# Early masks, the third pattern's copies and the last normalisation on ScalarE, and quarter turns in another order, in a hybrid encoder layer

## The chip, the cores and the metric

The kernel runs on one core of a Trainium2 chip. A core has five engines that matter here, each with its own queue that it works off in order: TensorE (PE; its weight loads are shown apart as PEld), VectorE (DVE), ScalarE (ACT), GpSimd (POOL) and SyncE (SP), which issues the DMAs. They wait for each other through semaphores. The metric is the device time of one execution in microseconds (us); a profile is one execution seen by the hardware profiler.

## The reference

One encoder layer on 2048 tokens of 1024 features, with three groups of heads. Cut to what matters:

```python
# A: 16 heads of 64, three dilation patterns (window, dilation), each a sliding window
DILATED_PATTERNS = ((128, 1), (512, 4), (2048, 16))
for window, dil in DILATED_PATTERNS:
    o, lse = window_attn(q[:, ::dil], k[:, ::dil], v[:, ::dil], n_side=window // (2 * dil))
out_A = sum(softmax(lse over the 3 patterns) * o)
# B: 8 heads of latent attention, dense over all 2048 keys
out_B = softmax((q_nope @ k_nope + q_rope @ k_rope) * scale) @ v
# M: 4 heads of cross-attention into 256 memory tokens
out_M = softmax(q @ k_mem * scale) @ v_mem
y = concat(RMSNorm_A(out_A), RMSNorm_B(out_B), RMSNorm_M(out_M)) * SiLU(gate)   # 2048 x 2048
h = LayerNorm(ALPHA * h + y @ W_out)                                             # 2048 x 1024
```

In the window attention a query sees the keys at most 64 places away in its subsequence; everything else is set to a large negative number before the softmax. The kernel does this with mask tiles.

## The kernel before, in words

Products that need more than half precision are made from a float16 high part and a float16 low part (`ph` and `pl`, `yh` and `yl`, `woh` and `wol`): the high part is a rounded copy, the low part a subtraction.

**Start, to 1367 us.** `embed` normalises the input and transposes it, then come the projections and gates, one long row of matmuls, and the memory attention.

**Dilated stage, about 1376 to 1757 us.** For each of 16 heads, `head_units` yields 10 units: four for the first pattern (`unit1`), four for the second (`unit2`), two for the third (`unit3`). A unit is a score tile of 128x1024 (a mask is added on PE by a product with `ident_b`, L1810, and the scores by L1819), one or two exponentials on ACT (`probabilities`, L1465 gives `pf`, L1476 or L1470 or DVE's L1472/L1478 gives `ph`), a subtraction for `pl` on DVE or POOL (L1473/L1479), edge masks on POOL (L1761), and the products with the values (`attend`, L1486 to L1488) into a PSUM tile `ps_o`, of which there are two. `Out.add` collects six row blocks in such a tile (at the end four) and copies it out (L1791) to the stage tile `so`, three copies to each pattern and head; a PSUM tile can be filled again only after its copy. `g` is the pattern, 0 to 2. The masks (`mask_tile`, `keep`, L1707 to L1736) are made by POOL: 5 memsets (L1708) and 28 affine selects (L1714), for the tiles `in`, `ed` (two each) and `diag`.

**Latent stage, 1757 to 2464 us.** For each of 8 heads and 4 query blocks (h, n) there are 8 units k2: six score matmuls (L1619 to L1621), two exponentials on ACT, `pl` on the engine that `lo_eng` picks (every third on POOL, else DVE), and 48 value matmuls; pairs of units are pushed together. Beside them run the maxima of a block to come: a matmul into `ps_x` (L1567) and a reduction on DVE (L1573) for each, two to a unit. At k2 = 6 of the blocks n = 1, 2, 3 of the first heads, `low` makes one 128x1024 piece of the output weight's low part on DVE (`wol`, L1984), 16 in all.

**Last stage, 2461 to 2846 us.** 16 output tiles of 128 tokens. `Prep` of a tile loads and merges the heads' results, takes the sums of squares (ACT, L2049), the roots (DVE, ACT, `rsqrt`) and normalises three groups of columns (`normalise`, L2060, DVE). `turn` then takes a quarter of 512 columns: four transposes on PE (L2068), the product with the gate (DVE, L2072), the high part (ACT, L2073) and the low part (DVE, L2074). Then 96 matmuls make the output tile (L2094), and `Post` adds the residual and normalises (L2142 to L2159).

The order of the work: in the latent and the last stage the code runs under `in_order`, so every engine's queue has the instructions in the order in which the code issues them, and the lists `planned` and `pipe` decide at which step a piece is issued. Outside such regions a scheduler places instructions; where the masks' instructions stand is its choice.

Of the kernel before, what the change touches and what calls it, by code (L numbers as in the profile page):

```python
# [16 lines left out]
ALU = mybir.AluOpType  # L17
# [45 lines left out]
def tile_layer(ctx: ExitStack, tc: tile.TileContext, x, mem, pos, invf, sgn, g_embT, b_embT, g_emb, b_emb, w_in,  # L63
# [175 lines left out]
    def value_block(vpool, chunks, vnat, unscale, dst, w, vt_bufs=1, both=False):  # L239


        amax = vpool.tile([P, NQ], F32, tag="vmx", name="v_amax")
        vt = vpool.tile([P, S], F32, tag="vt", bufs=vt_bufs, name="v_t")
        for n in range(NQ):
            ps = chunks(n)
            nc.scalar.activation(vt[:, n * 512:(n + 1) * 512], ps, AF.Copy, scale=w.un)
            nc.vector.tensor_reduce(out=amax[:, n:n + 1], in_=vt[:, n * 512:(n + 1) * 512], axis=AX.X, op=ALU.max,
                                    apply_absolute_value=True)
        am = vpool.tile([P, 4], F32, tag="vam", name="v_am")
        nc.vector.tensor_reduce(out=am[:, 0:1], in_=amax, axis=AX.X, op=ALU.max)  # L250
        nc.vector.tensor_scalar(out=am[:, 1:2], in0=am[:, 0:1], scalar1=1e-30, scalar2=None, op0=ALU.max)
        nc.vector.tensor_scalar(out=am[:, 0:1].bitcast(I32), in0=am[:, 1:2].bitcast(I32), scalar1=0x7F800000,
                                scalar2=None, op0=ALU.bitwise_and)
        nc.vector.tensor_scalar(out=am[:, 2:3], in0=am[:, 0:1], scalar1=2.0 ** -13, scalar2=None, op0=ALU.mult)
        nc.vector.reciprocal(am[:, 3:4], am[:, 2:3])
        nc.vector.tensor_copy(unscale, am[:, 2:3])
        vh = vpool.tile([P, S], F16, tag="vh", bufs=1, name="v_h")
        vl = vpool.tile([P, S], F16, tag="vl", bufs=1, name="v_l")
        for n in range(NQ):
            c = slice(n * 512, (n + 1) * 512)  # L260
            nc.scalar.activation(vh[:, c], vt[:, c], AF.Copy, scale=am[:, 3:4])
            nc.vector.scalar_tensor_tensor(out=vl[:, c], in0=vt[:, c], scalar=am[:, 3:4], in1=vh[:, c],
                                           op0=ALU.mult, op1=ALU.subtract)
        def turn(half, src, o):
            def go():
                pt = ps_x(F16)
                for i in range(8):
                    t = half * 8 + i
                    nc.tensor.transpose(pt[:, i * P:(i + 1) * P], src[:, t * P:(t + 1) * P], ident_h)
                vo, pv = vnat[:, half * 8:half * 8 + 8, :, o:o + 64], pt[:].rearrange("p (t h e) -> p t h e", t=8, h=2)  # L270
                if both and o == 0:
                    nc.vector.tensor_copy(vo, pv)
                else:
                    nc.scalar.copy(vo, pv)
                if half == 1 and o and dst is not None:
                    dst_t = dst.rearrange("(t p) c -> p t c", p=P)
                    nc.sync.dma_start(out=dst_t[:, 0:NT], in_=vnat[:].rearrange("p t h c -> p t (h c)"))
                    nc.sync.dma_start(out=dst_t[:, NT:], in_=vnat[:, 0:WRAP // P].rearrange("p t h c -> p t (h c)"))
            return go

        return [turn(half, src, o) for half in range(2) for src, o in ((vh, 0), (vl, 65))]


    early = ExitStack()
    sets, msets, vsets = [None, None], [None, None], [None, None]
    with ExitStack() as p1:
# [478 lines left out]
        with tc.tile_pool(name="nz", bufs=1, reuse_waits="tile", side="right") as nz, tc.tile_pool(name="sk", bufs=2, reuse_waits="tile", side="right") as sk:  # L765
            norms = nz.tile([P, 2, 8], F32, bufs=1, name="norms")
            powers = nz.tile([P, 2, 8], F32, bufs=1, name="powers")
            kscale = nz.tile([P, 8], F32, bufs=1, name="kscale")
            qscale = nz.tile([P, 8], F32, bufs=1, name="qscale")
            hbound = nz.tile([P, 1], F32, bufs=1, name="hbound")  # L770
            ones_b = nz.tile([P, 1], BF16, bufs=1, name="ones_b")
            same_head = nz.tile([P, P], F32, bufs=1, name="same_head")
            with tc.tile_pool(name="p0", bufs=1, side="right") as p0, in_order(*EALL):
                embed(p0)
            nc.sync.dma_start(out=gO, in_=g_outT)
            gain_powers()
            tables()
            plain(False, range(5, 8))
            with tc.tile_pool(name="ro", bufs=1, reuse_waits="tile", side="right") as ro:
                rotary(False)  # L780
                query_scales()
                with tc.tile_pool(name="sl", bufs=2, reuse_waits="tile", side="right") as sl:
                    plain(True, range(2, 8))
                    rotary(True)
# [809 lines left out]
    def latent_units(h):  # L1594
# [62 lines left out]
        for n in range(NQ):  # L1657
            for k2 in range(8):
                if (n, k2) == (0, 0 if h else 2):
                    begin()  # L1660
                if n and len(wol) < NT:
                    if k2 == 0:
                        raws.append(load_raw(la, len(woh), 1))
                    if k2 == 4:
                        high(raws[0])
                    if k2 == 6:
                        low(raws.pop())
                yield unit(n, k2)
# [13 lines left out]
                            ended.append((heads[h], m))  # L1682
                        yield

    lo_turn = [0]

    def lo_eng():
        lo_turn[0] += 1
        return nc.gpsimd if lo_turn[0] % 3 == 0 else nc.vector

    raws, planned = [], {}
# [10 lines left out]
    da = p3.enter_context(tc.tile_pool(name="da", bufs=2, reuse_waits="tile"))  # L1702
    ascale = da.tile([P, AH], F32, bufs=1, name="ascale")
    nc.sync.dma_start(out=ascale, in_=ascale_d)

    def mask_tile(name):
        t = da.tile([P, 512], BF16, bufs=1, name=name)  # L1707
        nc.gpsimd.memset(t, 0.0)  # L1708
        return t

    def keep(t, c0, shape, coef, base, cm):

        v = t[:, c0:c0 + shape[0] * shape[1]].rearrange("p (a b) -> p a b", a=shape[0])
        nc.gpsimd.affine_select(out=v, in_=v, pattern=[[coef[0], shape[0]], [coef[1], shape[1]]], base=base,  # L1714
                                channel_multiplier=cm, compare_op=ALU.is_ge, fill=NEG)

    masks = {}
    for pat, shape, coef in ((1, (16, 8), (1, 16)), (2, (4, 32), (1, 4))):
        neg = (-coef[0], -coef[1])
        inner = mask_tile(f"in{pat}")  # L1720
        edge = mask_tile(f"ed{pat}")
        for c0 in (0, 256):
            keep(inner, c0, shape, coef, 0, -1)
            keep(inner, c0 + 128, shape, neg, 0, 1)

        keep(edge, 0, shape, neg, 0, 1)
        keep(edge, 0, shape, (0, 0), -64, 1)
        keep(edge, 128, shape, coef, 0, -1)
        keep(edge, 128, shape, (0, 0), 63, -1)
        keep(edge, 256, shape, coef, 0, -1)  # L1730
        keep(edge, 384, shape, neg, 0, 1)
        masks[pat] = (inner, edge)
    diag = mask_tile("diag")
    for r in range(4):
        keep(diag, r * P, (1, P), (0, 1), 64, -1)
        keep(diag, r * P, (1, P), (0, -1), 64, 1)  # L1736


    W, STB = AH * 65, (2, 2, 1)
# [39 lines left out]
    class Out:  # L1779
# [3 lines left out]
        def add(self, items):  # L1783
# [4 lines left out]
            self.n += 1  # L1788
            if s == 5 or self.n == 16:
                k = self.n - self.lo  # L1790
                nc.vector.tensor_copy(self.stage[:, self.lo:self.n, 65 * self.e:65 * self.e + 65],  # L1791
                                      self.po[:, 0:65 * k].rearrange("p (t c) -> p t c", c=65))
                self.po = None
            if self.n == 16 and self.e == 1:
                store(self.pair, self.g, self.stage)
# [1 line left out]
    def head_units(pair, e, vals):  # L1797
# [86 lines left out]
        def unit3(g):  # L1884
            def scores():
                return score(8 + g, [([(P, slice(r, r + 16 * 127 + 1, 16), (lambda t, r=r: t[:, r * P:(r + 1) * P]))
                                for r in range(8 * g + 4 * b, 8 * g + 4 * b + 4)], diag) for b in range(2)])

            def values(pp):
                for i in range(8):  # L1890
# [67 lines left out]
    with ExitStack() as p4:  # L1958
# [29 lines left out]
        class Prep:  # L1988
# [68 lines left out]

            def normalise(self):
                for g, (a, b) in enumerate(self.GROUPS):
                    nc.vector.tensor_scalar(out=self.y[:, a:b], in0=self.y[:, a:b], scalar1=self.rs[:, g:g + 1], scalar2=None, op0=ALU.mult)  # L2060

        preps = [Prep(t) for t in range(NT)]

        def turn(t, q, pt):

            for i in range(4):
                k = 4 * q + i
                nc.tensor.transpose(pt[:, i * P:(i + 1) * P], y_of[t][:, k * P:(k + 1) * P], ident)  # L2068
            c = slice(512 * q, 512 * q + 512)
            yh, yl = ys[t % 2]  # L2070
            y = y_of[t][:, c]
            nc.vector.tensor_tensor(out=y, in0=pt, in1=gates[t][:, c], op=ALU.mult)  # L2072
            nc.scalar.copy(R(yh[:, c]), y)  # L2073
            nc.vector.tensor_tensor(out=R(yl[:, c]), in0=y, in1=yh[:, c], op=ALU.subtract)  # L2074

        HALVES = ((0, 512), (512, 1024))
        sums, done = {}, {}
# [213 lines left out]
```

## Time and profile before

| | us |
|---|---|
| median of three runs | 2851.88 |
| the three runs | 2843.26, 2851.88, 2852.86 |
| the profiled execution | 2848.22 |
| its span on the core | 2846.4 |
| PE busy in the span | 2664.6 |
| DVE busy | 1975.0 |
| ACT busy | 1562.9 |
| POOL busy | 919.8 |

The span is the time from the first to the last instruction in the profile; the profiled execution's own time is 1.8 us longer. A row of the timeline has the start, the time that the instruction took (or, with x4 at its end, that four of them took together), the engine, the line of the code, what is written and what is read; in brackets stands how long the engine had been idle before it and whose result ended that. In the table of waits, "PE ps_o L1486 <- DVE so L1791: 35.2, 42, 2.4" says that PE's instruction of line 1486 was held up 42 times by DVE's line 1791, 35.2 us in total and 2.4 us at most.

### The profile page before, as it was taken

The numbers are of one execution on the slowest core, as the hardware profiler recorded it, in microseconds if no ns is written. First come the engines' busy times: TensorE is split into PE (matmuls) and PEld (weight loads), VectorE is DVE, ScalarE is ACT, GpSimd is POOL, SyncE is SP. The second block draws the span as 40 slices with busy tenths as digits, with TensorE's granted clock in tenths as the row PEclk, the third lists the DMA queues.
The fourth block names the chain that finished last, engine by engine and source line by source line (L and its number), as shares of the span: only waits on it lengthen the run. The fifth ranks groups of instructions, "written<-read, shape, count | busy, mean of one in ns | idle before, by whom it ended". The sixth has DMA issues, their size and how long they took to land. (4 is left out here: it accounts for less than half of the span.)

```text
span 2846.4 us, 56965 instructions
## 1 busy us (share of the span) xinstructions
PE 2664.6 (94%) x22765; PEld 1596.8 (56%) x22765; DVE 1975.0 (69%) x4537; ACT 1562.9 (55%) x2104; POOL 919.8 (32%) x632
## 2 busy tenths in 40 slices
PE   7999999999999999999888888999999999899998
PEld 6644445545446675455577776555655555544444
DVE  7524244449993675744578888988888878588886
ACT  6645434442213565444578876878888878422221
POOL 4301013342224001212677775333333333222221
PEclk9999999999999999999999999999999999999999
DMA  5456335772324212467387777122212120366663
GB/s 170 145 172 187 100 103 159 173 191 80 97 75 148 67 58 67 143 200 227 114 182 182 205 155 135 38 58 64 68 44 61 27 65 13 102 177 179 172 179 96
DMA packets 280490, 347.32 MB, mean 122 GB/s; under 512 B 38816, under 2 KB 209056, under 8 KB 279200
## 3 DMA queue, kind: packets, MB, share of 16 engines
q1 hardware_dynamic: 280224, 343.69, 43.6%
q8 instruction: 178, 2.92, 0.4%
q14 instruction: 88, 0.72, 0.1%
HBM read 216.13 MB, written 127.45 MB: 121 GB/s over the span
## 5 line engine op out<-in xcount | busy, mean ns | idle before, releaser
L189 PE MATMUL ps_mm<-hT,w_h 128*128 128x512 f16 x2880 | 863.6, 382 | 5.4 <-ACT w_h L358 2.9
L189 PE MATMUL ps_mm<-hT,w_l 128*128 128x512 f16 x1440 | 547.5, 381 | 0.2 <-DVE w_l L362 0.2
L1479 POOL TENSOR_TENSOR pl<-pf,ph 128x1024 f16<-128x1024 f32 x117 | 299.5, 2560 | 466.8 <-ACT ph L1476 371.4
L189 PEld LDWEIGHTS <-w_h 128*128 128x128 f16 x2880 | 271.6, 99 | 277.3 <-issue 25.5
L1573 DVE TENSOR_REDUCE lmc<-ps_x 128x1 f32<-128x512 f32 x496 | 317.7, 682 | 92.7 <-PE ps_x L1567 92.3
L1465 ACT ACTIVATE pf<-ps_s,lscale 128x1024 f32<-128x1024 f32 x256 | 286.0, 1117 | 107.4 <-PE ps_s L1621 104.9
L1479 DVE TENSOR_TENSOR pl<-pf,ph 128x1024 f16<-128x1024 f32 x217 | 284.1, 1309 | 8.4 <-ACT ph L1476 7.3
L1476 ACT ACTIVATE ph<-ps_s,lscale 128x1024 f16<-128x1024 f32 x254 | 284.1, 1118 | 0.0
L1465 ACT ACTIVATE pf<-ps_s,shift_t,ascale 128x1024 f32<-128x1024 f32 x160 | 192.6, 1205 | 85.8 <-PE ps_s L1819 52.4
L189 PEld LDWEIGHTS <-w_l 128*128 128x128 f16 x1440 | 141.6, 98 | 172.6 <-issue 4.0
L1646 PE MATMUL ps_o<-lv,pl 128*128 128x65 f16 x2032 | 204.4, 194 | 4.6 <-POOL pl L1479 4.6
L1644 PE MATMUL ps_o<-lv,ph 128*128 128x65 f16 x2032 | 204.9, 194 | 0.0
L1645 PE MATMUL ps_o<-lv,ph 128*128 128x64 f16 x2032 | 204.7, 196 | 0.0
L1619 PE MATMUL ps_s<-hq,hq 97*128 97x512 f16 x512 | 198.0, 387 | 6.4 <-DMA hq<-lmr 3.4
L1644 PEld LDWEIGHTS <-ph 128*128 128x128 f16 x2032 | 190.4, 97 | 21.3 <-issue 10.0
L1645 PEld LDWEIGHTS <-ph 128*128 128x128 f16 x2032 | 190.5, 98 | 15.4 <-issue 0.8
L1620 PE MATMUL ps_s<-hq,hq 96*128 96x512 f16 x512 | 197.6, 386 | 0.0
L1621 PE MATMUL ps_s<-hq,hq 96*128 96x512 f16 x512 | 196.0, 383 | 0.0
L1646 PEld LDWEIGHTS <-pl 128*128 128x128 f16 x2032 | 190.2, 100 | 4.8 <-POOL pl L1479 4.7
L1819 PE MATMUL ps_s<-hq,hq 128*128 128x256 f16 (+3 forms) x1536 | 186.3, 259 | 0.0
L931 DVE CUSTOM_DVE_ANT_0 d1j<-ps_x,wm 128x256 bf16<-128x256 f32 (+1 forms) x608 | 184.5, 364 | 2.1 <-PE ps_x L928 1.4
L1567 PE MATMUL ps_x<-hq,hq 96*128 96x512 f16 x496 | 153.6, 382 | 21.6 <-DVE lmc L1573 21.4
(414 smaller groups left out, 5848.3 us busy)
## 6 DMA issues: line engine op xcount, KB each, us to landing
w_raw<-in_w_in_dram SPq DMA_DIRECT2D x56, 512.0 KB
oa<-oa_d SPq DMA_DIRECT2D x48, 520.0 KB
v<-va_d SPq DMA_DIRECT2D x24, 1032.0 KB
oa_d<-so SPq DMA_DIRECT2D x16, 1040.0 KB
gate_d<-sg SPq DMA_DIRECT2D x64, 256.0 KB
lv<-gate_d SPq DMA_DIRECT2D x15, 1024.0 KB
hq<-k_n SPq DMA_DIRECT2D x16, 576.0 KB
oa_d<-so SPq DMA_DIRECT2D x32, 260.0 KB
```

The lines of the kernel that those rows point to most:

```text
L189: nc.tensor.matmul(ps, R(a), R(b), start=(i == 0), stop=(i == n - 1))
L1465: nc.scalar.activation(pf, ps, AF.Exp, bias=bias, scale=scale)
L1476: nc.scalar.activation(ph, ps, AF.Exp, bias=bias, scale=scale)
L1479: pipe.later.append(lambda: lo_engine.tensor_tensor(out=pl, in0=pf, in1=ph, op=ALU.subtract))
L1573: nc.vector.tensor_reduce(out=self.mc[:, t % 4, n:n + 1], in_=ps, axis=AX.X, op=ALU.max)
L1619: nc.tensor.matmul(b, R(cur.kh[0:97, kc]), R(cur.qh[0:97, c]), start=True, stop=False)
L1620: nc.tensor.matmul(b, R(cur.kh[0:96, kc]), R(cur.ql[0:96, c]), start=False, stop=False)
L1621: nc.tensor.matmul(b, R(cur.kl[0:96, kc]), R(cur.qh[0:96, c]), start=False, stop=True)
L1644: nc.tensor.matmul(o, ph, v[:, 0:65], start=(k2 == 0 and j == 0 and i == 0), stop=False, skip_group_check=True)
L1645: nc.tensor.matmul(o[:, 0:64], ph, v[:, 65:129], start=False, stop=False, skip_group_check=True)
L1646: nc.tensor.matmul(o, pl, v[:, 0:65], start=False, stop=(k2 == 7 and j == 1 and i == 3), skip_group_check=True)
L1819: nc.tensor.matmul(o, kt[:, key], q, start=(i in bare and kt is ks and first), stop=(kt is kk and c0 == 512), skip_group_check=True)
```

## The change

Five edits. `build_masks` is called behind `embed`, and the mask tiles live in another pool. `Out.add` copies pattern 2 (the third) out on ScalarE. `lo_eng` sends the `pl` of units 6 and 7 to POOL in the blocks in which `low` runs, and starts its count of three again there. `normalise` runs on ScalarE for all tiles but the first. `turn` issues the low part of a quarter behind the gate product of the next one, and the last quarter's behind that.

```diff
@@ behind the masks' helpers, moved up; mask_tile now allocates from cpool @@
+    masks = {}
+
+    def build_masks():
+        for pat, shape, coef in ((1, (16, 8), (1, 16)), (2, (4, 32), (1, 4))):
...
+            masks[pat] = (inner, edge)
+        diag = masks[3] = mask_tile("diag")
...
                 embed(p0)
             nc.sync.dma_start(out=gO, in_=g_outT)
             gain_powers()
+            build_masks()
             tables()
...
                     if k2 == 4:
                         high(raws[0])
+                    busy[0] = 2 * (k2 == 6) or busy[0]
                     if k2 == 6:
                         low(raws.pop())
                 yield unit(n, k2)
...
-    lo_turn = [0]
+    lo_turn, busy = [0], [0]
 
     def lo_eng():
         lo_turn[0] += 1
+        if busy[0]:
+            busy[0] -= 1
+            lo_turn[0] = 0
+            return nc.gpsimd
         return nc.gpsimd if lo_turn[0] % 3 == 0 else nc.vector
...
-                nc.vector.tensor_copy(self.stage[:, self.lo:self.n, 65 * self.e:65 * self.e + 65],
-                                      self.po[:, 0:65 * k].rearrange("p (t c) -> p t c", c=65))
+
+                (nc.scalar.copy if self.g == 2 else nc.vector.tensor_copy)(
+                    self.stage[:, self.lo:self.n, 65 * self.e:65 * self.e + 65], self.po[:, 0:65 * k].rearrange("p (t c) -> p t c", c=65))
...
             def normalise(self):
                 for g, (a, b) in enumerate(self.GROUPS):
-                    nc.vector.tensor_scalar(out=self.y[:, a:b], in0=self.y[:, a:b], scalar1=self.rs[:, g:g + 1], scalar2=None, op0=ALU.mult)
+                    if self.t:
+                        nc.scalar.activation(self.y[:, a:b], self.y[:, a:b], AF.Copy, scale=self.rs[:, g:g + 1])
+                    else:
+                        nc.vector.tensor_scalar(out=self.y[:, a:b], in0=self.y[:, a:b], scalar1=self.rs[:, g:g + 1], scalar2=None, op0=ALU.mult)
...
+            yh, yl = ys[t % 2]
+
+            def low(q):
+                c = slice(512 * q, 512 * q + 512)
+                nc.vector.tensor_tensor(out=yl[:, c], in0=y_of[t][:, c], in1=yh[:, c], op=ALU.subtract)
+
             c = slice(512 * q, 512 * q + 512)
-            yh, yl = ys[t % 2]
             y = y_of[t][:, c]
             nc.vector.tensor_tensor(out=y, in0=pt, in1=gates[t][:, c], op=ALU.mult)
-            nc.scalar.copy(R(yh[:, c]), y)
-            nc.vector.tensor_tensor(out=R(yl[:, c]), in0=y, in1=yh[:, c], op=ALU.subtract)
+            nc.scalar.copy(yh[:, c], y)
+
+            if q:
+                low(q - 1)
+            if q == 3:
+                low(3)
```

How the queues move at the three places that the prediction speaks of. POOL at the very start of the program, in the changed kernel (L285 and L291 are the masks' memsets and selects, L718 is the first subtraction of `embed`, L684 before):

```order
L433 AFFINE_SELECT same_head<-same_head 128x128
L291 AFFINE_SELECT in_1541<-in_1541 128x128 x4
L291 AFFINE_SELECT ed_1543<-ed_1543 128x128 x4
L285 MEMSET in_1575 128x512
...
L516 AFFINE_SELECT pick<-pick 128x16
L291 AFFINE_SELECT ed_1577<-ed_1577 128x128 x2
L291 AFFINE_SELECT diag<-diag 128x128 x4
L516 AFFINE_SELECT pick<-pick 128x16
L718 TENSOR_TENSOR hT_133<-hf,hT_133 128x2x256 x8
```

The call stands behind `embed` in the code, but the scheduler put all 33 instructions ahead of `embed`'s first one on POOL; before they stood in front of the dilated stage.

DVE around the second `wol` piece, before:

```order
L1577 TENSOR_REDUCE lmx<-lmc 128x4
L1984 SCALAR_TENSOR_TENSOR wol_23147<-wo_raw,fw,woh_23057 128x1024
L1573 TENSOR_REDUCE lmc<-ps_x 128x1 x2
L1479 TENSOR_TENSOR pl<-pf,ph 128x1024
L1573 TENSOR_REDUCE lmc<-ps_x 128x1 x2
```

and in the changed kernel (L1612 is `lmx`, L1993 `wol`, L1608 the reductions, L1514 `pl`):

```order
L1612 TENSOR_REDUCE lmx<-lmc 128x4
L1514 TENSOR_TENSOR pl<-pf,ph 128x1024
L1993 SCALAR_TENSOR_TENSOR wol_23147<-wo_raw,fw,woh_23057 128x1024
L1608 TENSOR_REDUCE lmc<-ps_x 128x1 x8
L1514 TENSOR_TENSOR pl<-pf,ph 128x1024
```

The two `pl` behind `wol` have left DVE, and one `pl` now stands right in front of it. The count of three, which ran on through all blocks, now begins anew in each block with a `wol`. Counted over the 16 pieces: the place "`pl` of unit 4 on DVE, that of unit 5 on POOL, then `wol`, then four or more reductions in a row" came 6 times before, and comes 10 times in the changed kernel.

DVE in a tile of the last stage, in the changed kernel (L2089 is the gate product, L2085 the low part, L2163 and L2165 the residual):

```order
L167 TENSOR_TENSOR rsg<-rs_y_36616,rs_t_36622 128x3
L2089 TENSOR_TENSOR lv_21578<-ps_o,lv_21579 128x512 x2
L2085 TENSOR_TENSOR yl_33938<-lv_21578,yh_33937 128x512
L2089 TENSOR_TENSOR lv_21578<-ps_o,lv_21579 128x512
L2085 TENSOR_TENSOR yl_33938<-lv_21578,yh_33937 128x512
L2089 TENSOR_TENSOR lv_21578<-ps_o,lv_21579 128x512
L2085 TENSOR_TENSOR yl_33938<-lv_21578,yh_33937 128x512 x2
L2163 SCALAR_TENSOR_TENSOR ht<-ht,fsc,ps_s 128x512
```

Before, three normalising instructions stood between the first row and the products, and products and low parts took turns one by one. On ACT the third pattern's copies stand behind the exponentials of the next head's first unit (one copy) and second unit (two copies).

More of the change, by code (lines that the diff above doesn't have):

```diff
@@ L281, in value_block, with mask_tile, keep @@
         return [turn(half, src, o) for half in range(2) for src, o in ((vh, 0), (vl, 65))]
+    def mask_tile(name):
+        t = cpool.tile([P, 512], BF16, bufs=1, name=name)
+        nc.gpsimd.memset(t, 0.0)
+        return t
+    def keep(t, c0, shape, coef, base, cm):
+        v = t[:, c0:c0 + shape[0] * shape[1]].rearrange("p (a b) -> p a b", a=shape[0])
+        nc.gpsimd.affine_select(out=v, in_=v, pattern=[[coef[0], shape[0]], [coef[1], shape[1]]], base=base,
+                                channel_multiplier=cm, compare_op=ALU.is_ge, fill=NEG)
+    masks = {}
+    def build_masks():
+        for pat, shape, coef in ((1, (16, 8), (1, 16)), (2, (4, 32), (1, 4))):
+            neg = (-coef[0], -coef[1])
+            inner = mask_tile(f"in{pat}")
+            edge = mask_tile(f"ed{pat}")
+            for c0 in (0, 256):
+                keep(inner, c0, shape, coef, 0, -1)
+                keep(inner, c0 + 128, shape, neg, 0, 1)
+            keep(edge, 0, shape, neg, 0, 1)
+            keep(edge, 0, shape, (0, 0), -64, 1)
+            keep(edge, 128, shape, coef, 0, -1)
+            keep(edge, 128, shape, (0, 0), 63, -1)
+            keep(edge, 256, shape, coef, 0, -1)
+            keep(edge, 384, shape, neg, 0, 1)
+            masks[pat] = (inner, edge)
+        diag = masks[3] = mask_tile("diag")
+        for r in range(4):
+            keep(diag, r * P, (1, P), (0, 1), 64, -1)
+            keep(diag, r * P, (1, P), (0, -1), 64, 1)
     early = ExitStack()
@@ L1704, in tile_layer @@
     nc.sync.dma_start(out=ascale, in_=ascale_d)
[L1706 to L1736, printed above, removed]
     W, STB = AH * 65, (2, 2, 1)
@@ L1886, in scores @@
                 return score(8 + g, [([(P, slice(r, r + 16 * 127 + 1, 16), (lambda t, r=r: t[:, r * P:(r + 1) * P]))
-                                for r in range(8 * g + 4 * b, 8 * g + 4 * b + 4)], diag) for b in range(2)])
+                                for r in range(8 * g + 4 * b, 8 * g + 4 * b + 4)], masks[3]) for b in range(2)])
             def values(pp):
```

## The prediction

> **What bounds the kernel now.** I read the page first, then the waits of TensorE, then the stages one by one.
>
> ```profile
> span 2846.4 us, 56965 instructions
> PE 2664.6 (94%) x22765; PEld 1596.8 (56%) x22765; DVE 1975.0 (69%) x4537; ACT 1562.9 (55%) x2104; POOL 919.8 (32%) x632
> ```
>
> PE is busy for 2664.6 of 2846.4 us, so no more than 181.8 us can be won without taking matmuls away, and the change takes none. What it can win are PE's waits:
>
> ```profile
> PE ps_o L1486 <- DVE so L1791: 35.2, 42, 2.4
> PE ps_x L1567 <- DVE lmc L1573: 21.4, 18, 2.5
> PE ps_o L2068 <- DVE lv L2060: 20.1, 14, 4.6
> PE ps_o L1488 <- POOL pl L1473: 11.2, 24, 0.6
> PE ps_s L1810 <- POOL ed L1714: 8.6, 1, 8.6
> PE ps_o L1646 <- POOL pl L1479: 4.6, 1, 4.6
> ```
>
> Each edit aims at one of these rows, and their own sum, 101.1 us, is the ceiling. By stage (columns: length; busy time of PE, PEld, DVE, ACT, POOL; granted clock):
>
> ```profile
> 1400.00:1757.00 357.00, 306.32 (x5177) 265.30 (x5174) 293.19 (x358) 278.06 (x277) 272.73 (x238) 0.99 0.74 169
> 1757.00:2464.00 707.00, 674.15 (x8416) 407.20 (x8415) 587.96 (x823) 567.66 (x581) 243.75 (x101) 0.97 0.20 53
> 2500.00:2800.00 300.00, 286.43 (x1418) 141.66 (x1417) 252.00 (x422) 68.87 (x148) 70.92 (x38) 1.00 0.61 177
> ```
>
> In the dilated stage PE stands idle for 14% and four engines are near their limit; in the other two it is nearly full, and DVE (83%, 84%) comes next.
>
> **1. The masks.**
>
> ```profile
> 1366.93 0.38 PE L189 MATMUL ps_mm<-hT,w_l 128*128 128x512 f16 x1
> 1375.89 0.58 PE L1810 MATMUL ps_s<-ed,ident_b 128*128 128x512 bf16 x1 [8.59 <-POOL ed L1714]
> 1381.33 0.38 PE L1810 MATMUL ps_s<-in,ident_b 128*128 128x512 bf16 x1
> 1367.43 2.01 POOL L1253 MEMSET hq<- 1x2304 f16 x1 [18.34 <-PE ps_mm L189]
> 1369.52 1.53 POOL L1714 TENSOR_SCALAR_AFFINE_SELECT in<-in 128x128 bf16<-128x128 bf16 x4
> 1376.86 1.06 POOL L1714 TENSOR_SCALAR_AFFINE_SELECT diag<-diag 128x128 bf16<-128x128 bf16 x4
> ```
>
> POOL can begin the selects only behind a memset that waits for the last projections, and PE waits 8.59 us. Then PE runs at about half speed (0.58 against 0.38 for the same 128x512 matmul) for some 5 us. With the masks there, PE could begin right behind the projections; I leave 0.7 for the hand-over and add 1.6 for the slow matmuls (of 2.4 at the most, since exponentials follow): **-9.5**. Bounds: -7 (another load is late, no clock gain) to -10.5.
>
> At the program's start POOL has room:
>
> ```profile
> 14.91 1.16 POOL L684 TENSOR_TENSOR hT<-hf,hT 128x512 f16<-128x512 f32 x1 [12.30 <-ACT hT L683]
> ```
>
> The selects took 1369.5 to 1377.9, 8.4 us; five memsets of 0.53 make it 11.1 at most. POOL is idle from 14.91 - 12.30 = 2.61; from there they end before 13.7, and 1.2 us of the idle 12.30 are left. If the selects slow DVE's first work there, PE's start moves by it. Bounds 0 to +2.5; I take **+0.8**.
>
> **2. The third pattern's copies.** A head boundary:
>
> ```profile
> 1571.48 2.12 POOL L1479 TENSOR_TENSOR pl<-pf,ph 128x1024 f16<-128x1024 f32 x1 [0.63 <-ACT ph L1476]
> 1571.61 3.07 DVE L1473 TENSOR_TENSOR pl<-pf,ph 128x1024 f16<-128x1024 f32 x1
> 1574.61 0.89 DVE L1791 COPY so<-ps_o 128x390 f32<-128x390 f32 x2
> 1575.21 0.19 PE L1486 MATMUL ps_o<-v,ph 128*128 128x65 f16 x1 [1.34 <-DVE so L1791]
> 1577.19 1.21 ACT L1465 ACTIVATE pf<-ps_s,shift_t,ascale 128x1024 f32<-128x1024 f32 x1 [2.08 <-PE ps_o L1488]
> L1791 DVE COPY so<-ps_o 128x390 f32<-128x390 f32 x88 | 48.6, 552 | 41.8 <-PE ps_o L1488 41.8
> L1791 DVE COPY so<-ps_o 128x260 f32<-128x260 f32 x45 | 18.6, 412 | 0.0
> ```
>
> A subtraction of 3.07 us (others take 1.2) stands ahead of the copy, and PE waits 1.34 for its PSUM tile. On ACT the three copies of a head would take some 0.57, 0.57 and 0.44 (estimate, by columns from the 512-wide L789 row below and the 1024-wide exponential), 1.58 in all; DVE loses 0.55 + 0.55 + 0.41 = 1.51.
>
> ```profile
> L789 ACT ACTIVATE sg<-ps_mm,fun 128x512 f32<-128x512 f32 x64 | 44.0, 687 | 224.5 <-PE ps_mm L189 158.7 <-issue 43.5 <-DMA gate_d<-sg 21.5
> ```
>
> ACT has 357 - 278.06 = 79 us idle over 15 heads, 5.3 each, 2.08 of it in one piece just before the copies' neighbours. But in ACT's queue a copy stands between exponentials and waits for PE's value products; behind it stand the next exponentials, which POOL's masks and `pl` wait for. Walking one head by hand, the exponentials of its second and third unit come 1.2 to 1.5 later, the POOL subtraction too, which no longer lies beside DVE's, and the first value products come 1.46 sooner; but the next pattern's copies on DVE move by 0.1 to 0.6 only, and PE meets them again. I take 0.7 a head, 16 x 0.7 = **-11**. Bounds: 16 x 1.34 = -21 (that wait gone), +25 (16 x 1.58, all of it on the path).
>
> **3. Units 6 and 7 on POOL.**
>
> ```profile
> L1984 DVE SCALAR_TENSOR_TENSOR wol<-wo_raw,fw,woh x16: 1275/1752/3155, 1805.6 to 2225.5; 128x1024 f16<-128x1024 f32 x16
> 1909.88 2.73 POOL L1479 TENSOR_TENSOR pl<-pf,ph 128x1024 f16<-128x1024 f32 x1 [4.74 <-PE ps_x L1581]
> 1910.54 3.15 DVE L1984 SCALAR_TENSOR_TENSOR wol<-wo_raw,fw,woh 128x1024 f16<-128x1024 f32 x1
> 1914.35 0.38 PE L1567 MATMUL ps_x<-hq,hq 96*128 96x512 f16 x1 [2.15 <-DVE lmc L1573]
> 1914.95 0.38 PE L1567 MATMUL ps_x<-hq,hq 96*128 96x512 f16 x1 [0.22 <-DVE lmc L1573]
> 1932.52 1.27 DVE L1984 SCALAR_TENSOR_TENSOR wol<-wo_raw,fw,woh 128x1024 f16<-128x1024 f32 x1
> 1852.00:1855.00 3.00, 3.00 (x26) 1.68 (x24) 1.04 (x1) 0.00 (x0) 0.00 (x0) 0.50 1.05 240
> ```
>
> The 16 `wol` take from 1.28 to 3.15. All the long ones have a POOL `pl` that began about 0.7 to 1.1 earlier, that of unit 5; DVE's reductions come late and PE loses 2.15 + 0.22 = 2.37. There are six such places, and after four of them, as behind 1850, PE's clock falls to 0.50 for some 3 us: about 1.6 lost each time, 1.1 on the mean of the six. In the change the two `pl` *behind* `wol` go to POOL, but that of unit 5, which is the one that collides, is sent to POOL in ten of the sixteen blocks instead of six, because the count begins anew. In those ten DVE meets `wol` with the same work ahead of it as in the six. 4 more x (2.37 + 1.1) = **+14**. Bounds: +9 (no clock loss) to +23 (longer waits, since POOL then has three `pl` in a row).
>
> Those three in a row may make the value products of units 6 and 7 wait: POOL takes 2.3 to 2.7 for a `pl` and a unit takes 2.5, so the last ends about 0.2 late; and at the stage's end the phases of the count move around the 4.6 us wait for a POOL `pl` above. **+2.5**, bounds -2 to +6.
>
> **4. The last stage.** PE's row for L2060 has 20.1 us in 14 waits; the longest, 4.64, is the first tile's, whose chain comes from a load and stays. The other 13 have 15.5, 1.2 each. One tile on DVE:
>
> ```profile
> 2544.09 1.54 DVE L2060 TENSOR_SCALAR lv<-lv,rsg 128x1024 f32<-128x1024 f32 x3
> 2526.34 0.69 DVE L2074 TENSOR_TENSOR yl<-lv,yh 128x512 f16<-128x512 f32 x1 [0.68 <-ACT yh L2073]
> DVE yl L2074 <- ACT yh L2073: 35.6, 52, 0.7
> 2544.99 0.63 PE L2068 MATMUL ps_o<-ident,lv 128*128 128x128 f32 x4 [0.72 <-DVE lv L2060]
> 2569.03 0.63 PE L2068 MATMUL ps_o<-ident,lv 128*128 128x128 f32 x4 [1.38 <-DVE lv L2060]
> L2049 ACT ACTIVATE junk<-lv 128x1024 bf16<-128x1024 f32 x16 | 16.9, 1056 | 36.5 <-POOL lv L2036 36.5
> ```
>
> From one tile's first transposes to the next are 24.04 us. DVE waits 4 x 0.68 = 2.7 us in it for the high parts; with the low part one quarter later these waits are filled, and 2.0 remain as gain (the last quarter still waits once). The normalising takes 1.54 off DVE and puts 1.06 for the first group on ACT (as the L2049 row) ahead of the transposes. DVE's loop becomes 24.04 - 2.0 - 1.54 + 1.06, and some 0.6 for the two hand-overs to ACT and back: 22.2, below PE's 24.04 - 1.38 = 22.7. PE sets the pace, and nearly all of the 15.5 goes. ACT has 231 of 300 us free there. **-13**, bounds -15.5 to -5.
>
> A rule of the Trainium skill speaks against this edit: "ScalarE: Activation LUTs", section "Rules for kernel authors", has multiplications done on VectorE, not on ScalarE, because VectorE needs less time per element. The rows agree on the single operation, and by the rule alone the stage would lose the difference on each tile instead of winning; that case has a price of its own as rival D.
>
> **The sum.** -9.5 + 0.8 - 11 + 14 + 2.5 - 13 = -16.2. The profiled execution took 2848.2 (span 2846.4 and 1.8 around it), which gives 2832.0; the median of the three runs lies 3.7 above it. I take half of that, since one of the three lies 5 us below the profiled run: 2834.
>
> **The rivals.**
>
> A, slower: the dilated copies hold up the exponentials. The place is ACT's queue, where the copy waits for PE's products. It decides when the exponentials behind it come later than ACT's idle 2.08 can take in; then all 1.58 of each head come on top: +25 in place of -11, 2834 + 36 = 2870. For it: POOL waits 57 us for `pf` in this stage (row below), so a late exponential has a customer. Against: the walk gains at the first gate.
>
> ```profile
> POOL pf L1761 <- ACT pf L1465: 57.0, 33, 4.3
> ```
>
> B, nothing won in the dilated stage: the copies of the first pattern stay on DVE and stay the gate. 2834 + 11 = 2845. For it: they make up most of the 42 waits.
>
> C, the `wol` collisions vanish, because POOL's three `pl` move in time or DVE, rid of two `pl`, catches up: -6 x 3.5 = -21 in place of +14, 2834 - 35 = 2799. Against: the work ahead of `wol` is the same as in the six.
>
> D, normalising on ACT lengthens the chain of a tile, if its length and not DVE's load sets the pace: 1.06 + 0.62 + 0.62 = 2.30 there (estimate: the wide row above, and the narrow ones somewhat below the 0.69 of the L789 row) against 1.54 on DVE, 14 x 0.76 = +11 in place of -13, 2834 + 24 = 2858. Against: DVE's 35.6 us of waits go in any case.
>
> That the masks are not early is ruled out by POOL's order; that their cover at the start fails is in the bounds of part 1.
>
> **How the numbers follow.** Forecast 0.43, A 0.15, B 0.22, C 0.12, D 0.08. About 0.5%, 14 us, is what a measurement of this kernel can tell from no change: faster means below 2837.6, slower above 2866. The forecast stands near the first bound: 0.33 of it faster, 0.10 same. C counts as faster (0.12), B 0.17 same and 0.05 faster, D 0.07 same and 0.01 slower, A 0.12 slower and 0.03 same: faster 0.50, same 0.37, slower 0.13. The forecast's own range, from the spread of the terms, is 2820 to 2850; to hold 8 in 10 it reaches to 2805 and 2860.
>
> **What would show it.** The L1810 wait of 8.6 gone, and L684's first start still at 14.9. Ten `wol` of 3.15 and ten PE waits above 2 at L1567 (now six). The L1486 row falling from 35.2 to about 24, with a new row from ACT's copies. The L2068 row down to about 6. What would make me wrong first: fewer than ten long `wol`, or L1486's wait moving onto ACT whole.

## The result, and the profile after

| | us |
|---|---|
| changed kernel, median of 4 runs | 2826.38 (2823.95 to 2828.96) |
| kernel before, median of 4 runs | 2849.29 (2843.26 to 2852.86) |
| ratio | 0.9922, interval 0.9907 to 0.9937 |
| span of the profiled execution | 2825.1 (before 2846.4) |

The change makes the kernel 0.8% faster, 18 to 27 us; 2834 was forecast, 18 below the median of 2851.88 that was known then. The page of the changed kernel and the waits of its TensorE:

```profile
span 2825.1 us, 56944 instructions
PE 2666.0 (94%) x22765; PEld 1604.6 (57%) x22765; DVE 1926.0 (68%) x4427; ACT 1612.3 (57%) x2197; POOL 970.1 (34%) x649
```

```profile
PE ps_x L1602 <- DVE lmc L1608: 30.7, 25, 2.1
PE ps_o L1521 <- DVE so L1800: 30.0, 31, 2.1
PE ps_x L709 <- DVE xt L696: 12.0, 8, 7.7
PE ps_o L1681 <- POOL pl L1514: 7.4, 1, 7.4
PE ps_o L1523 <- POOL pl L1508: 4.6, 11, 0.4
PE ps_o L2080 <- ACT lv L2070: 3.0, 1, 3.0
```

The line numbers have moved: L1602 was L1567, L1521 was L1486, L1523 was L1488, L1681 was L1646, L2080 was L2068. Four of the six rows aimed at have shrunk or gone: the wait for the masks (8.6) is no longer there, that at the last stage's transposes has gone from 20.1 to 3.0 and is one tile's alone, that for POOL's `pl` in the dilated stage from 11.2 to 4.6, that for the copies from 35.2 to 30.0. Two have grown: the latent stage's maxima, 21.4 to 30.7, and the one wait for a POOL `pl` at its end, 4.6 to 7.4. By stage, in the windows used before:

```profile
1400.00:1757.00 357.00, 316.17 (x5281) 271.44 (x5278) 302.98 (x333) 303.30 (x333) 284.10 (x238) 0.99 0.78 175
1757.00:2464.00 707.00, 664.78 (x8203) 403.27 (x8203) 556.45 (x786) 553.11 (x568) 275.88 (x113) 0.96 0.19 50
2500.00:2800.00 300.00, 300.00 (x1495) 149.96 (x1494) 235.33 (x416) 104.53 (x198) 71.46 (x38) 1.00 0.61 178
```

PE is busier in the dilated window (316 for 306), less busy in the latent one (665 for 674) and without any gap in the last one (300 of 300). But the stages of the changed kernel begin up to 22 us earlier, so the first two windows no longer hold the same work. I therefore also read from both timelines when PE begins four things, and took the lengths between them:

| from ... to | before | after | difference |
|---|---|---|---|
| start to the first transposes | 11.49 | 12.39 | +0.90 |
| to the first mask product | 1364.40 | 1355.63 | -8.77 |
| to the first score matmul of the latent stage | 387.89 | 373.34 | -14.55 |
| to the second tile's first transposes | 708.69 | 727.81 | +19.12 |
| to the end | 373.96 | 355.96 | -18.00 |

The sum is -21.3, the two spans' difference. The latent stage has given back about half of what the other parts won. These are one execution each, and the second row is the least exact: it is mostly projections that the change leaves alone, and among the kernels below that do not wait for the masks it lies anywhere from 1352.6 to 1364.3.

### The profile page after: what moved, and what is told of

It is laid out like the page before. It is cut to its first block, busy times and chain, and to the rows that moved or that the text cites. A ratio compares the mean times of both kernels' runs of the same rounds, so it can differ in the third digit from the quotient of the medians.

```text
span 2825.1 us, 56944 instructions
## 1 busy us (share of the span) xinstructions
PE 2666.0 (94%) x22765; PEld 1604.6 (57%) x22765; DVE 1926.0 (68%) x4427; ACT 1612.3 (57%) x2197; POOL 970.1 (34%) x649
## 4 chain that ended last, share of the span: by engine, by line
PE 45%; DVE 9%; issue 4%; DMA 4%; ACT 3%; POOL 2%; SPq 0%; DVEq 0%; ACTq 0%; POOLq 0%
PE ps_s L2115 10%; PE ps_mm L189 6%; PE ps_x L1602 3%; PE ps_s L1654 3%; PE ps_s L1655 3%; PE ps_s L1656 3%; PE ps_o L1680 2%; PE ps_o L1681 2%; PE ps_o L1679 2%; PE ps_x L189 2%; PE ps_s L1828 2%; DVE lmc L1608 2%; PE ps_x L2115 1%; ACT pf L1500 1%; DVE pl L1514 1%
## 5 line engine op out<-in xcount | busy, mean ns | idle before, releaser
L1514 POOL TENSOR_TENSOR pl<-pf,ph 128x1024 f16<-128x1024 f32 x134 | 342.1, 2556 | 450.1 <-ACT ph L1511 368.0
L1608 DVE TENSOR_REDUCE lmc<-ps_x 128x1 f32<-128x512 f32 x496 | 318.3, 684 | 123.8 <-PE ps_x L1602 122.8
L1514 DVE TENSOR_TENSOR pl<-pf,ph 128x1024 f16<-128x1024 f32 x200 | 270.8, 1355 | 4.7 <-ACT ph L1511 1.9
L1681 PE MATMUL ps_o<-lv,pl 128*128 128x65 f16 x2032 | 211.5, 197 | 7.4 <-POOL pl L1514 7.4
L1679 PE MATMUL ps_o<-lv,ph 128*128 128x65 f16 x2032 | 212.3, 197 | 0.0
L1680 PE MATMUL ps_o<-lv,ph 128*128 128x64 f16 x2032 | 211.9, 199 | 0.0
L1679 PEld LDWEIGHTS <-ph 128*128 128x128 f16 x2032 | 194.5, 99 | 22.1 <-issue 10.7
L1680 PEld LDWEIGHTS <-ph 128*128 128x128 f16 x2032 | 194.8, 100 | 16.0 <-issue 2.0
L1681 PEld LDWEIGHTS <-pl 128*128 128x128 f16 x2032 | 194.4, 102 | 7.7 <-POOL pl L1514 7.6
L1602 PE MATMUL ps_x<-hq,hq 96*128 96x512 f16 x496 | 154.7, 384 | 30.8 <-DVE lmc L1608 30.7
```

The source lines that it names most:

```text
L1514: pipe.later.append(lambda: lo_engine.tensor_tensor(out=pl, in0=pf, in1=ph, op=ALU.subtract))
L1608: nc.vector.tensor_reduce(out=self.mc[:, t % 4, n:n + 1], in_=ps, axis=AX.X, op=ALU.max)
L1679: nc.tensor.matmul(o, ph, v[:, 0:65], start=(k2 == 0 and j == 0 and i == 0), stop=False, skip_group_check=True)
L1680: nc.tensor.matmul(o[:, 0:64], ph, v[:, 65:129], start=False, stop=False, skip_group_check=True)
L1681: nc.tensor.matmul(o, pl, v[:, 0:65], start=False, stop=(k2 == 7 and j == 1 and i == 3), skip_group_check=True)
```

## The experiments

The theory was the prediction's: each part acts in its own stage, and the parts add up. The rival: they act through each other, and the latent stage is longer because it is entered in another phase.

### One part at a time

**Masks alone** (`build_masks()` behind `gain_powers()` as in the diff, nothing else of it).

```diff
             gain_powers()
+            build_masks()
             tables()
```

> The kernel before with the masks made early and nothing else. Theory: the parts stand by themselves, and this one is worth what the two traces differ by at its place: PE's 8.6 us wait at the dilated stage's first mask product goes, the first transposes come 0.9 later, 7 to 9 us faster in all (a little more if the half clock behind the wait goes too). Rival: the parts act together, and the dilated stage gives part of it back, since its head-by-head waits are set by other engines: 0 to 4 us faster.

Measured: ratio 0.9966 (0.9952 to 0.9980), 10 us faster, between 6 and 14. The wait of 8.6 us for the masks is gone, and the other waits of the dilated stage are not smaller than before (37.1 us for the copies, before 35.2; 12.4 for POOL's `pl`, before 11.2). The rival's 0 to 4 us is ruled out.

**The copies alone.**

```diff
-                nc.vector.tensor_copy(self.stage[...], ...)
+                (nc.scalar.copy if self.g == 2 else nc.vector.tensor_copy)(self.stage[...], ...)
```

> The kernel before with the third pattern's copies on ScalarE and nothing else. Theory: per head PE's waits fall from 3.3 to 2.4 us, 16 x 0.9 = 14 us faster, and the latent stage keeps its six long wol. Rival: the gain in the changed kernel came from the earlier start and the shifted phase, and the copies alone give 0 to 5 us.

Measured: 0.9942 (0.9922 to 0.9962), 16 us faster, between 11 and 22. They need neither the masks nor the new phase.

**Units 6 and 7 on POOL alone.**

```diff
+                    busy[0] = 2 * (k2 == 6) or busy[0]
...
+        if busy[0]:
+            busy[0] -= 1
+            lo_turn[0] = 0
+            return nc.gpsimd
```

> The kernel before with units 6 and 7 on POOL and the count begun anew, and nothing else. Theory: ten long wol instead of six and one half-clock window behind nearly each, 4 x 3.7 = 15 to 20 us slower. Rival: the latent stage of the changed kernel is longer because of what comes before it (copies, masks), and this part alone changes nothing or helps by taking 32 subtractions off DVE: -5 to +3.

Measured: 1.0080 (1.0059 to 1.0101), 23 us slower, between 17 and 29. The latent stage is 728.3 long, in the changed kernel 727.8, before 708.7; there are ten `wol` of 3.15 us. The rival falls: this part lengthens the stage by itself.

**The last stage's two edits alone** (`normalise` and `turn` as in the diff).

```diff
+                    if self.t:
+                        nc.scalar.activation(self.y[:, a:b], self.y[:, a:b], AF.Copy, scale=self.rs[:, g:g + 1])
...
+            if q:
+                low(q - 1)
+            if q == 3:
+                low(3)
```

> The kernel before with the last stage's two edits (normalise on ScalarE, low part one quarter later) and nothing else. Theory: PE's waits at the transposes go but for the first, 14 to 18 us faster. Rival: part of the 18 us that the traces show from the second tile's turn to the end came from the end of the latent stage having moved: 8 to 12 us.

Measured: 0.9941 (0.9918 to 0.9964), 17 us faster, between 10 and 23. From the second tile's turn to the end it is 18.6 us shorter than before, so the gain is the stage's own.

The four together make 10 + 16 - 23 + 17 = 20 us; the change as a whole made 22. Each of the four is known to 4 to 6 us only, so by the times alone an interaction of some 10 us could hide in the sum. The traces are sharper. The latent stage lasts 728.3 us with the units alone and 727.8 in the changed kernel (708.7 before), the last one 355.4 with its two edits alone and 356.0 (374.0 before), the dilated one 368.8 with the copies alone and 373.3 (387.9 before). So each part acts in its own stage, and they add up to within some 5 us.

### Which half of the last stage

**Only the low parts later; only the normalising moved.**

```diff
-            nc.vector.tensor_tensor(out=R(yl[:, c]), in0=y, in1=yh[:, c], op=ALU.subtract)
+            if q:
+                low(q - 1)
+            if q == 3:
+                low(3)
```

> The kernel before with only the low parts one quarter later, the normalising still on VectorE. Theory: DVE's loop over a tile, 24.0 us, sets the pace of the last stage; it falls by 2.0 to 22.0, below PE's 22.7, so this half alone wins nearly all, 13 to 17 us. Rival: the chain through the normalising sets the pace, the low parts lie behind it, and this half wins 0 to 5 us.

```diff
-                    nc.vector.tensor_scalar(out=self.y[:, a:b], in0=self.y[:, a:b], scalar1=self.rs[:, g:g + 1], scalar2=None, op0=ALU.mult)
+                    if self.t:
+                        nc.scalar.activation(self.y[:, a:b], self.y[:, a:b], AF.Copy, scale=self.rs[:, g:g + 1])
+                    else:
+                        nc.vector.tensor_scalar(out=self.y[:, a:b], in0=self.y[:, a:b], scalar1=self.rs[:, g:g + 1], scalar2=None, op0=ALU.mult)
```

> The kernel before with only the normalising on ScalarE, the low parts as before. Theory: DVE's loop falls from 24.0 by 1.54 less the 1.06 and the hand-overs that come into the chain, so 0 to 0.5 us a tile, 0 to 7 us faster. Rival (dearer operation on ScalarE decides): 14 x 0.76 = 11 us slower. Other rival: it is this half that matters, 10 to 15 us faster.

Measured: the low parts alone 0.9935 (0.9915 to 0.9955), 18 us faster; the normalising alone 1.0004 (0.9986 to 1.0021), nothing. PE's waits with the low parts alone, and below it those with the normalising alone:

```profile
PE ps_o L2068 <- DVE lv L2060: 4.1, 1, 4.1
```

```profile
PE ps_o L2071 <- ACT lv L2061: 19.5, 14, 4.6
```

The 20.1 us before became 4.1 in one wait with the low parts moved. With the normalising moved they stayed, 19.5 in 14 waits, and only bear another engine's name. What ScalarE takes for it, in the groups by line and shape of that kernel, and below it VectorE in the last stage of the kernel before:

```profile
L2061 ACT ACTIVATE lv<-lv,rsg 128x512 f32<-128x512 f32 x30 | 19.8, 707 | 0.0
L2061 ACT ACTIVATE lv<-lv,rsg 128x1024 f32<-128x1024 f32 x15 | 17.2, 1147 | 16.7 <-DVE rsg L167 16.7
```

```profile
L2060 DVE TENSOR_SCALAR lv<-lv,rsg 128x512 f32<-128x512 f32 x30 | 13.2, 481 | 0.0
L2060 DVE TENSOR_SCALAR lv<-lv,rsg 128x1024 f32<-128x1024 f32 x15 | 11.3, 754 | 1.6
```

1.15 and 0.71 against 0.75 and 0.48 on VectorE. The work left VectorE, but the wait for its result stayed in the same chain (roots, normalising, transposes, gate product), and each link is dearer. That single operations are dearer on ScalarE is what the Trainium skill, "ScalarE: Activation LUTs", section "Rules for kernel authors", says of multiplications. It gives its factor for bf16; these float32 rows agree in direction, at about 1.5. It cost the stage no time.

### None, six, ten and sixteen collisions

If a `wol` that meets a POOL `pl` is what lengthens the latent stage, its length must follow the number of such meetings. Both kernels are the changed one with a fixed choice in the blocks that make a `wol` (the comment stands for the second kernel's line and is not in the code):

```diff
+    def lo_eng(h, n, k2):
+        if fixed.get((h, n)):
+            lo_turn[0] = k2
+            return nc.gpsimd if k2 in (0, 3, 6) else nc.vector   # the other kernel: (2, 5, 6, 7)
...
+            fixed[h, n] = n and len(wol) < NT
```

> The changed kernel, in which the 16 blocks with a wol send the pl of units 0, 3 and 6 to POOL and no others, so that none runs when wol does. Theory: no wol of 3.15 (all 1.28), ten waits of 2.1 to 2.4 and their half-clock windows gone, 10 x 3.7 = 32 to 40 us faster than the changed kernel, that is 50 to 62 faster than before. Rival: the time goes to other waits (with two pl more on DVE the reductions get late anyway): 0 to 15 us faster than the changed kernel.

> The changed kernel, in which all 16 blocks with a wol send units 2, 5, 6 and 7 to POOL, so that every wol meets the pl of unit 5. Theory: 16 wol of 3.15, six collisions more than in the changed kernel, 6 x 3.7 = 18 to 26 us slower than it, about level with before. Rival: the 3.15 is no matter of the neighbour on POOL but of the block's place: no change against the changed kernel, within 5 us.

Measured against the kernel before: 0.9785 (0.9769 to 0.9800) with none, that is about 39 us faster than the changed kernel; 1.0001 (0.9992 to 1.0010) with all sixteen, about 23 us slower than it (both through the ratios to the kernel before, so good to some 6 us). The `wol` (name, least, median and longest ns) with none and with all:

```profile
L1992 DVE SCALAR_TENSOR_TENSOR wol<-wo_raw,fw,woh x16: 1276/1278/1280, 1776.4 to 2177.5; 128x1024 f16<-128x1024 f32 x16
```

```profile
L1992 DVE SCALAR_TENSOR_TENSOR wol<-wo_raw,fw,woh x16: 3148/3151/3154, 1786.5 to 2246.7; 128x1024 f16<-128x1024 f32 x16
```

| collisions | latent stage, us | PE's gaps in it | the rest |
|---|---|---|---|
| 0 | 688.0 | 21.6 | 666.4 |
| 6 (before) | 708.7 | 31.8 | 676.9 |
| 10 (changed) | 727.8 | 43.3 | 684.5 |
| 16 | 750.1 | 58.9 | 691.2 |

(A collision is a `wol` of 3.15; the kernel before has five more of 1.75, behind which TensorE has no wait. The length runs from the first score matmul to the second tile's first transposes; the rest is the length less the gaps.) The rest grows because matmuls run at half clock: the clock records of the two traces have 3 half-clock stretches in this length with none and 19 with all, which cost 10.2 and 37.5 us. From 0 to 16 the stage grows by 62.1 us, 3.9 for each collision: 2.3 of gap and 1.6 of slow clock. The rows between are less exact. Six other kernels of this series with six long `wol` have a stage of 700.0 to 706.5, so the 708.7 of the kernel before is at the long end. So the rival that the time moves to other waits falls, and so does the one that the place and not the neighbour matters.

### What the copies do, and three attempts to go on

**Only the second of the three copies on ScalarE** (kernel before).

```diff
+                (nc.scalar.copy if self.g == 2 and self.lo == 6 else nc.vector.tensor_copy)(...)
```

> The kernel before with only the second of the third pattern's three copies on ScalarE. Theory: this is the copy that stands behind the 3.07 us subtraction and holds PE 1.34 us a head; it alone brings most of the part's gain, 9 to 14 us, and PE's wait of 1.34 at the start of the next head's value products is gone. Rival: the gain comes from taking all three off VectorE's queue (1.5 us a head), and one alone gives a third, 3 to 6 us.

Measured: 0.9969 (0.9955 to 0.9983), 9 us faster, between 5 and 13: at the theory's lower end, about half of what all three bring. The interval also overlaps the rival's 3 to 6, so the time does not decide between them. Its waits in the whole run:

```profile
PE ps_o L1486 <- DVE so L1792: 17.1, 29, 1.5
PE ps_o L1488 <- POOL pl L1473: 11.2, 24, 0.6
PE ps_o L1488 <- DVE pl L1473: 10.9, 13, 1.0
```

The 1.34 us wait of each head is gone from the first row (35.2 before), but behind it comes a new one of 0.81 for the long subtraction itself, the third row. That subtraction stays with one copy moved and goes with three: VectorE has 13 of over 3 us on this line before, 13 here, and 2 with all three copies moved.

**Late masks, normalising back, a fourth copy.** All three are the kernel without collisions with the masks built at the end of the value projections; the second has `normalise` on VectorE again, the third has one copy more on ScalarE.

```diff
-            build_masks()
...
             nc.sync.dma_start(out=un_a.rearrange("o (b p) -> (o b) p", p=P), in_=ub)
+            build_masks()
```

> The kernel of e7 (no wol collides) with the masks built later, at the end of the value projections, in POOL's order as written. Theory: PE's first transposes start at 11.5 again instead of 11.9 to 12.4, 0.4 to 0.9 us faster than e7, too little for the times to tell, but seen in the wait at the first transposes, and the masks still cause no wait at the dilated stage. Rival: the 33 instructions slow VectorE wherever they stand, and PE waits in the value projections instead: 0 to 8 us slower than e7.

```diff
-                    if self.t:
-                        nc.scalar.activation(self.y[:, a:b], self.y[:, a:b], AF.Copy, scale=self.rs[:, g:g + 1])
```

> The kernel of e10 with the normalising back on VectorE for all tiles. Theory: the low parts' new place is the whole gain of the last stage, so this is the same within 2 us. Rival: with the low parts moved, VectorE's loop is near PE's pace, and 1.54 us more a tile brings PE's waits back, 5 to 10 us slower than e10.

```diff
+                (nc.scalar.copy if self.g == 2 or (self.g == 0 and self.lo == 6) else nc.vector.tensor_copy)(...)
```

> The kernel of e10 with one copy more on ScalarE in each head, the second of the first pattern, for which PE still waits 1.4 us a head. Theory (ScalarE has little room left between its exponentials, some 3 us a head in small pieces): the exponentials behind that copy come later, and the gain is small, -8 to +5 against e10. Rival: every copy taken off VectorE removes its wait, 16 x 1.4 = 18 to 22 us faster than e10.

Measured: 0.9780 (0.9765 to 0.9794), 0.9774 (0.9757 to 0.9791) and 0.9786 (0.9769 to 0.9803) of the kernel before: the same as each other and as the kernel without collisions. With the late masks PE begins its first transposes at 11.50 again (7.72 us of waiting in the changed kernel):

```profile
11.50 0.48 PE L709 MATMUL ps_x<-ident,xt 128*128 128x128 f32 x1 [6.84 <-DVE xt L696]
```

With the normalising back on VectorE, PE still has no gap in 260 us of the last stage:

```profile
2480.00:2740.00 260.00, 260.00 (x1295) 130.13 (x1294) 219.96 (x398) 64.18 (x141) 66.75 (x35) 1.00 0.64 186
```

With the fourth copy PE's wait for copies falls from 29 us to 7.9, but the subtractions behind it take its place:

```profile
PE ps_o L1523 <- POOL pl L1508: 18.7, 29, 0.7
PE ps_o L1523 <- DVE pl L1508: 9.3, 17, 1.8
PE ps_o L1521 <- DVE so L1799: 7.9, 16, 0.6
```

In the profile of the kernel without collisions the first and third rows are 5.1 and 29.2. The sum stays: 35.9 here, and 5.1 + 2.8 + 29.2 = 37.1 there. So not every copy off VectorE is a gain; whether ScalarE's later exponentials or something else delays those subtractions was not told apart.

The kernels without collisions beat both kernels of this case: about 2783 us where the kernel before took about 2845 beside them, 2.2% below it and 1.4% below the changed one.

## Why the prediction was right

| term | predicted | from the two traces | as a part alone |
|---|---|---|---|
| masks, with the start | -8.7 | -7.9 | -10 (-14 to -6) |
| third pattern's copies | -11 | -14.6 | -16 (-22 to -11) |
| units 6 and 7 on POOL | +16.5 | +19.1 | +23 (+17 to +29) |
| last stage | -13 | -18.0 | -17 (-23 to -10) |
| sum | -16.2 | -21.3 | -20 |

Every term has its sign and lies within four tenths of its size.

**The masks.** The hand-over and the price at the start came out as worked out. The selects keep POOL busy to 14.1, PE's first transposes move from 11.49 to 12.39 (+0.8 predicted), and PE steps from the last projection straight into the mask product:

```profile
1367.81 0.38 PE L189 MATMUL ps_mm<-hT,w_l 128*128 128x512 f16 x1
1368.02 0.38 PE L1819 MATMUL ps_s<-ed,ident_b 128*128 128x512 bf16 x1
12.46 1.51 POOL L291 TENSOR_SCALAR_AFFINE_SELECT diag<-diag 128x128 bf16<-128x128 bf16 x4
15.80 1.16 POOL L718 TENSOR_TENSOR hT<-hf,hT 128x512 f16<-128x512 f32 x1 [1.67 <-ACT hT L717]
```

The granted clock is 1.00 from 1368 to 1374, where before it was 0.60 from 1376 to 1382, so the slow matmuls behind the wait are gone too. My sign that `embed`'s first subtraction would stay at 14.9 was wrong by the same 0.9: it is at 15.80. That the selects' place is the cause is shown by the late masks, with which the 0.9 goes.

**The copies.** The size was a third too small, and one step of the picture was wrong. I expected a new wait for ScalarE's copies; PE's table has none. I also expected the row for the copies to fall to 24; it is 30.0, and more of the gain stands in another row, POOL's `pl`, 11.2 to 4.6. Together these are 11.8 of the 14.6 (kernels without the copies differ by 4 us among themselves in this stage). In each head PE's waits were 0.55, 1.34, 0.42, 0.38 and 0.58, together 3.3; now they are 1.41, 0.42 and 0.55, together 2.4. The 1.34 that the walk removed did go, and the 1.41 is a copy of the first pattern:

```profile
1563.82 1.23 DVE L1508 TENSOR_TENSOR pl<-pf,ph 128x1024 f16<-128x1024 f32 x1
1565.07 0.42 DVE L1304 COPY hq<-hq 64x512 f16<-64x512 f16 x1
1565.41 0.88 DVE L1800 COPY so<-ps_o 128x390 f32<-128x390 f32 x2
1566.01 0.19 PE L1521 MATMUL ps_o<-v,ph 128*128 128x65 f16 x1 [1.41 <-DVE so L1800]
```

That PE meets the next pattern's copies again, as predicted, is this row: it meets one, and three small waits dissolve into it. The copies are also cheaper on ScalarE than my 0.57:

```profile
L1800 ACT COPY so<-ps_o 128x390 f32<-128x390 f32 x32 | 15.6, 488 | 20.5 <-PE ps_o L1523 20.5
```

The walk also noted, and did not price, that POOL's subtraction no longer lies beside VectorE's. The 3.07 us row of the head boundary is such a meeting: POOL's subtraction ends at 1571.48 + 2.12 = 1573.60 and VectorE's at 1574.68, 1.08 later. Before, 26 of VectorE's 95 subtractions of this stage are lengthened in this way, to between 2.4 and 3.1 us, and every one ends 1.08 after POOL's; in the changed kernel it is 16, and VectorE spends 141 us on all 95 instead of 158. With only the second copy moved it is 26 and 158 again, and half the gain. That the other half comes from the meetings fits these counts, but the meetings were not varied by themselves here.

Rival A, that the exponentials come late by all of it, and rival B, that nothing is won, are both ruled out by the copies alone; the fourth copy shows rival B's mechanism one step further on.

**Units 6 and 7.** The count of ten, the mechanism and its price held:

```profile
L1993 DVE SCALAR_TENSOR_TENSOR wol<-wo_raw,fw,woh x16: 1278/3148/3153, 1780.9 to 2219.7; 128x1024 f16<-128x1024 f32 x16
1917.16 0.38 PE L1602 MATMUL ps_x<-hq,hq 96*128 96x512 f16 x1 [2.15 <-DVE lmc L1608]
1918.00:1921.00 3.00, 3.00 (x50) 2.74 (x49) 0.90 (x2) 0.00 (x0) 2.86 (x3) 0.50 0.94 217
```

The median has become the long form, and behind the wait PE runs at 0.50 for some 3 us. What was too small is the clock's share: I took four slow windows for six collisions, 1.1 each; here nine of ten bring one, and over the series it is 1.6. With that, 4 x 2.3 + 10 x 1.55 - 6 x 1.1 = 18 instead of 14. Against the six other kernels with six long `wol` the stage is 21 to 28 us longer, not 19, which is nearer to the 23 of the part alone. The smaller term, +2.5, came out at +2.8, but by one of its two reasons only: the value products of units 6 and 7 have no wait behind three `pl` in a row, and all of it is the one wait at the stage's end, 4.6 to 7.4.

The rows also say why the length of `wol` takes just three values. Before, the subtraction on POOL that began at 1909.88 ended at 1912.61, and `wol` at 1913.69, 1.08 later. In another block:

```profile
1887.72 2.32 POOL L1479 TENSOR_TENSOR pl<-pf,ph 128x1024 f16<-128x1024 f32 x1 [5.24 <-ACT ph L1476]
1889.37 1.75 DVE L1984 SCALAR_TENSOR_TENSOR wol<-wo_raw,fw,woh 128x1024 f16<-128x1024 f32 x1
```

POOL ends at 1890.04 and `wol` at 1891.12, again 1.08 later, though it had begun 0.67 before POOL's end and not 2.07. The same 1.08 stands behind all eleven meetings of the kernel before (six long and five of 1.75), all ten of the changed one and all sixteen of the kernel with sixteen. So `wol` does its work (1.08 of the 1.28 us that it takes alone) only once POOL has finished, whenever it starts. The Trainium skill, "SBUF — State Buffer", section "SBUF: two separate sides", says that a VectorE operation with two inputs in SBUF and a GpSimd operation that reads SBUF exclude each other for a whole instruction; these rows and the sixteen of 3.15 agree.

**The last stage.** The gain lies at -18.0, beyond my bound of -15.5, because the one wait that I kept whole went from 4.64 to 3.0; 0.9 is not in PE's waits, and I have not traced it. I called that wait the first tile's. It stands at 2497.16, one tile behind the second tile's first transposes at 2472.47, so it is the third's. The tiles behind it now follow each other every 22.5 us (PE's 22.7 in the prediction).

What I did not see is that the sum gives the normalising no worth: it takes 1.54 off VectorE's loop and puts 1.06 and 0.6 back. The low parts' waits, 2.0 a tile, were enough alone to bring the loop from 24.0 to 22.0, under PE's 22.7. The runs say the same: the normalising is worth nothing alone (1.0004), and nothing where the low parts have moved (0.9780 with it, 0.9774 without). The rule against ScalarE (rival D) did not cost 11 us either; the interval of the normalising alone ends at 6 us slower. Why it costs nothing even alone can be read in its trace:

```profile
2545.71 0.69 DVE L2075 TENSOR_TENSOR lv<-ps_o,lv 128x512 f32<-128x512 f32 x1 [2.07 <-PE ps_o L2071]
2547.09 1.39 DVE L2077 TENSOR_TENSOR yl<-lv,yh 128x512 f16<-128x512 f32 x1 [0.68 <-ACT yh L2076]
```

From the end of the roots to the first gate product of a tile VectorE now waits 2.07 us, where before it spent 1.67, of which 1.54 normalising: 0.40 more, in every tile from the fourth on. But the four products and low parts behind it take 8.73 us on the mean of these tiles instead of 9.07, mostly because the first low part takes 1.42 instead of 1.70. Where that low part meets a POOL instruction on `oa` it ends 0.55 behind it, in both kernels, so this looks like a meeting of the same kind, and here it happened to get shorter.

## What to carry to other kernels

Count meetings, not instructions: an operation that gets off a busy engine helps only if it does not lengthen another one that meets it, and here the choice of the two units *behind* the critical one decided, through a counter begun anew, where the one *beside* it ran. A hand-over inside a chain (product, rounding on another engine, subtraction) was filled here with the next piece's work, and that won what moving an operation to another engine did not. And the price of one stage's wait was measured by setting its cause to none and to all: the two ends gave the price of a collision, 3.9 us, and the better kernel with it.

## What was not expected of the hardware

Behind a wait of TensorE of 2.1 us its granted clock fell to half, for 3.4 us at the least, in nine of ten collisions of the changed kernel and in all sixteen of the kernel with sixteen, and so made a collision dearer by 1.6 us than its gap. In the kernels with six collisions it was three to five of the six; what decides was not told apart. And the whole matter is narrow: a subtraction on POOL that starts 1.65 us before `wol` costs it 0.47 us and TensorE nothing, one that starts 0.7 us before costs it 1.87 us and TensorE 3.9 on the mean.
